# Order of the split products inside a tile of expert weights: high parts of both row halves first, then the low parts

## Chip, cores and metric

The kernel runs on one core of a Trainium2 chip. The metric is the device time of one execution in microseconds (us), given as the median of several runs. The core's engines are TensorE (PE, matrix products; PEld are its weight loads), VectorE (DVE), ScalarE (ACT), GpSimd (POOL) and SyncE (SP, which here issues DMAs).

## What is computed

The reference is one transformer block: modulation, a token mixer (neighbourhood attention beside a recurrent branch), a normalisation, and a mixture of experts with expert choice routing. The change touches the experts alone. Cut to them:

```python
N_EXPERTS = 16; CAPACITY_FACTOR = 2; D_EXPERT = 2816   # T = 1024 tokens, d = 1024
def expert_choice_ffn(u, w_router, w1, w3, w2):
    cap = CAPACITY_FACTOR * T // N_EXPERTS                # 128 tokens per expert
    aff = jax.nn.softmax(u @ w_router, axis=-1)
    gate, idx = lax.top_k(jnp.swapaxes(aff, 1, 2), cap)
    xs = jax.vmap(lambda ub, ib: ub[ib])(u, idx)
    hdn = silu(einsum('becd,edf->becf', xs, w1)) * einsum('becd,edf->becf', xs, w3)
    ye = einsum('becf,efd->becd', hdn, w2) * gate[..., None]
    return scatter_add(ye, idx)
```

Each of the 16 experts has 128 tokens, two up projections of 1024 x 2816 and one down projection of 2816 x 1024, all in float32.

## The kernel before

**Tiling.** The expert stage is the function `moe`. The 2816 hidden columns of an expert are cut into three chunks `FC` of 1024, 1024 and 768 columns. A step is one chunk of one matrix: (e, ci, 1) for `w1`, (e, ci, 3) for `w3`, (e, ci, 2) for `w2`. The down step of a chunk stands one chunk late, after the two up steps of the next. A step is cut into units, each of two blocks of 128 rows of the weight ("row halves", k = 2q and 2q+1): four units for an up step, four (or three, for 768) for a down step. That makes 35 units per expert and 560 in all. An up unit of the last chunk is 768 columns wide, the others are 1024 wide.

**From memory to the products.** `load(u)` (L878) issues the DMA of unit u into one of 13 `raw` buffers on SP's queue. `split(u)` writes the weights as a sum of two tiles: ScalarE casts the high part `hi` (L884), and VectorE subtracts it from `raw` to get the low part `lo` (L885). `hi` and `lo` each come from a ring of three buffers (`HLB=3`), and a buffer is free again when its last reader is done. The activations are split in the same way, into `xh` and `xl` for the up steps and `dh` and `dl` for the down steps. A product is then three matmuls: high by high, high activation by low weight, and low activation by high weight. The weight tile is the moving operand, the activation block of 128 x 128 is the stationary one, and a row of 1024 columns makes two matmuls of 512 (for 768, one of 512 and one of 256). So a unit is twelve matmuls: L986 for the up steps, into the accumulators `ph`, and L1001 for the down steps, into `ye`.

**Around the products.** After the last unit of a `w1` step ScalarE takes SiLU of `ph` into `hd` (L989), after `w3` VectorE multiplies `hd` (L991). TensorE transposes `hd` (L1023), ScalarE and VectorE split it into `dh` (L1024) and `dl` (L1025). At the end of an expert VectorE scales `ye` into `yo` (L1006), and GpSimd adds it into `acc` in memory (L1008). During an expert the next one is prepared: one-hot rows `oh` (L826), token numbers `idx` (L832), a gather, transposes (L850) and the split of the activations (L853 to L857). Near the end of the last expert `final(t)` (L947 to L971) normalises and stores the output rows on ScalarE, VectorE and GpSimd.

**What sets the order.** The program is written unit by unit: splits two units ahead (`LA`), loads twelve ahead (`LD`), then the unit's matmuls. A planner in the compiler places the instructions of each engine by the program's order and its own estimate of when inputs and buffers are ready. Each engine then runs its list in that fixed order.

Of the kernel before, what the change touches and what calls it, by code (L numbers as in the profile page):

```python
# [98 lines left out]
def ln_stats(nc, pool, t, mh_t, eps=LN_EPS, at=None):  # L99

    st=pool.tile([128,2,6],F32,name="bst",bufs=3) if at is None else at[:,:12].rearrange("p (s c) -> p s c",s=2)
    for s in range(2): nc.vector.bn_stats(st[:,s,:], t[:,s*512:(s+1)*512])
    mv=pool.tile([128,4],F32,name="bmv",bufs=3) if at is None else at[:,12:16]
    nc.vector.bn_aggr(mv[:,0:2], st)
    nc.vector.tensor_scalar_add(mv[:,2:3], mv[:,1:2], eps)
    nc.gpsimd.tensor_tensor(mv[:,3:4], mv[:,2:3], mh_t, op=ALU.pow)
    return mv[:,0:1], mv[:,3:4]
# [628 lines left out]
def moe(ctx, tc, K, get_t1, mc, i, G, out):  # L736
    nc=tc.nc
# [28 lines left out]
    with ExitStack() as c1:  # L766
# [6 lines left out]
        for t in range(NT):  # L773
            r=slice(t*128,(t+1)*128)
            x=get_t1(t,p)
# [16 lines left out]
            st=nc.sync.dma_start(table[r,:D],x)  # L792
# [28 lines left out]
    NC_=len(FC)  # L821

    def prep(e):
        oh=ep.tile([128,NT,128],BF16,name="oh",bufs=1)
        for t in range(NT):
            oi=nc.vector.tensor_scalar(oh[:,t,:],iota,slotT[:,t,e:e+1],None,op0=ALU.is_equal)  # L826
            if e in (1,2): behind(P[0]["xi"],oi)
        pi=ps_t.tile([128,4,128],F32,name="pt")
        for t in range(NT):
            for j in range(2): nc.tensor.matmul(pi[:,0,:1],oh[:,t,:],tok[:,t,j:j+1],start=(t+j==0),stop=(t+j==NT))  # L830
        idx=ep.tile([128,1],I32,name="idx",bufs=3)
        ic=nc.vector.tensor_copy(idx,pi[:,0,:1])  # L832
        g=ep.tile([128,D+NE],F32,name="gath",bufs=1)
        gi=nc.gpsimd.indirect_dma_start(out=g,out_offset=None,in_=table[:,:],  # L834
            in_offset=bass.IndirectOffsetOnAxis(ap=idx[:,:1],axis=0))
        return dict(gi=gi,ic=ic,idx=idx,g=g,e=e)
# [32 lines left out]
    def load(u,after=None):  # L869
        z,q=U[u]; e,ci,m=steps[z]; f0,fw=FC[ci]  # L870
        if m==2: ap,w=w2[e,f0+q*256:f0+q*256+256,:],D
        else: ap,w=(w1 if m==1 else w3)[e,q*256:q*256+256,f0:f0+fw],fw
        j=len(RN)%(RAW0+RAWB+RAW2); RN.append(0)
        z=G["raw0"] if j<RAW0 and u<len(U)-FS+LD else raw if j<RAW0+RAWB else raw2
        if len(RN)==1: r=G["r0"]
        else:
            r=z.tile([128,2048],F32,name="raw")
            di=(nc.gpsimd if after else nc.sync).dma_start(r[:,:2*w].rearrange("p (n w) -> p n w",n=2),ap.rearrange("(k p) f -> p k f",p=128))  # L878
            if after: behind(after,di)
        SP[u]=(r,w)  # L880
    def split(u):
        r,w=SP[u]
        hi,lo=[hl.tile([128,2048],F32R,name=n) for n in ("hi","lo")]
        nc.scalar.copy(hi[:,:2*w],r[:,:2*w])  # L884
        li=nc.vector.tensor_sub(lo[:,:2*w],r[:,:2*w],hi[:,:2*w].bitcast(F32))  # L885
        if u<12: behind(P[0]["ic"],li)
        SP[u]=[(hi[:,k*w:(k+1)*w],lo[:,k*w:(k+1)*w]) for k in range(2)]
    with tc.tile_pool(name="m2",bufs=2,side="right") as p:
# [34 lines left out]
        w=lambda n: p.tile([128,2,128],F32,name=n,bufs=1)  # L923
# [22 lines left out]
    def scale_shift(x,nm,rs,op):  # L946
        nc.vector.scalar_tensor_tensor(x,x,nm,g2row,op0=op,op1=ALU.mult)  # L947
        nc.vector.scalar_tensor_tensor(x,x,rs,b2row,op0=ALU.mult,op1=ALU.add)
# [25 lines left out]
    for u,(s,q) in enumerate(U):  # L974
        e,ci,m=steps[s]; last=q==nu(ci,m)-1
        for n in range(SN,min(u+LA+1,len(U))): split(n); SN=n+1
        if u+LD<len(U): load(u+LD)
        d=P[e]; w=SP.pop(u); f0,fw=FC[ci]; nf=fw//128
        if m!=2:
            if q==0: PH[m]=[ps_h.tile([128,512],F32,name=f"ph{m}{j}") for j,_ in halves(fw)]  # L980
            xh,xl=d["xh"],d["xl"]
            for k in (2*q,2*q+1):
                wh,wl=w[k%2]
                for x,y,a,b in ((xh,wh,True,False),(xh,wl,False,False),(xl,wh,False,True)):
                    for j,c in halves(fw):
                        nc.tensor.matmul(PH[m][j][:,:c.stop-c.start],x[:,k,:],y[:,c],start=(k==0 and a),stop=(k==7 and b))  # L986
            if last and m==1:
                hd=ep.tile([128,1024],F32,name="hd",bufs=1)
                for j,c in halves(fw): nc.scalar.activation(hd[:,c],PH[1][j][:,:c.stop-c.start],AF.Silu)  # L989
            elif last:  # L990
                for j,c in halves(fw): nc.vector.tensor_mul(hd[:,c],hd[:,c],PH[3][j][:,:c.stop-c.start])  # L991
                HD[e,ci]=hd
        else:
            if ci==0 and q==0: YE[e]=[ps_y.tile([128,512],F32,name=f"ye{j}") for j in range(2)]
            ye=YE[e]; dh,dl=DH[e,ci]
            for k in (2*q,2*q+1):
                st=(ci==0 and k==0); sp=(ci==NC_-1 and k==nf-1)
                wh,wl=w[k%2]
                for l,rr,a,b in ((dh,wh,True,False),(dh,wl,False,False),(dl,wh,False,True)):
                    for j in range(2):  # L1000
                        nc.tensor.matmul(ye[j],l[:,k,:],rr[:,j*512:(j+1)*512],start=st and a,stop=sp and b)  # L1001
            if ci==NC_-1 and last:
                yo=ep.tile([128,D],F32,name="yo",bufs=1)
                for j in range(2):
                    c=slice(j*512,(j+1)*512)
                    nc.vector.scalar_tensor_tensor(yo[:,c],ye[j],d["gate"],gt2row[:,c],op0=ALU.mult,op1=ALU.mult)  # L1006
                if e<NE-1:
                    nc.gpsimd.indirect_dma_start(out=acc[:,:],out_offset=bass.IndirectOffsetOnAxis(ap=d["idx"][:,:1],axis=0),  # L1008
                        in_=yo,in_offset=None,compute_op=ALU.add)
                else:  # L1010
                    nc.vector.tensor_add(yo,yo,ag);
                    nm,rs=ln_stats(nc,None,yo,mh,at=Q[:,0,:16])
                    scale_shift(yo,nm,rs,ALU.subtract)

        nxt=steps[s+1] if s+1<len(steps) else None
        for key in list(HD) if last else ():
            if m==2 or (m==3 and (nxt is None or nxt[2]!=2)) or (nxt==(key[0],key[1],2)):
                ee,cc=key; fw2=FC[cc][1]; nf2=fw2//128
                hd=HD.pop(key)
                dh=ep.tile([128,8,128],F32R,name="dh",bufs=1); dl=ep.tile([128,8,128],F32R,name="dl",bufs=1)  # L1020
                for k0 in range(0,nf2,4):
                    n=min(4,nf2-k0); ks=slice(k0,k0+n); pt=ps_t.tile([128,4,128],F32,name="pt")
                    for k in range(n): nc.tensor.transpose(pt[:,k,:],hd[:,(k0+k)*128:(k0+k+1)*128],ident)  # L1023
                    nc.scalar.copy(dh[:,ks],pt[:,:n])  # L1024
                    nc.vector.tensor_sub(dl[:,ks],pt[:,:n],dh[:,ks].bitcast(F32))  # L1025
                DH[key]=(dh,dl)
        if last and m==1 and ci==0 and e+1<NE: P[e+1]=prep(e+1)
        if q==1 and m!=2 and ci==NC_-1 and e+1<NE: prep2(P[e+1],(m//2,))
        if u==len(U)-FS:
            ag=ep.tile([128,D+NE],F32,name="gath",bufs=1)[:,:D]  # L1030
            nc.gpsimd.indirect_dma_start(out=ag,out_offset=None,in_=acc[:,:],in_offset=bass.IndirectOffsetOnAxis(ap=P[NE-1]["idx"][:,:1],axis=0))
            gb=G["raw0"].tile([128,2048],F32,name="raw"); g2row,b2row=gb[:,:D],gb[:,D:]
            for z,n in ((g2row,2),(b2row,3)): nc.sync.dma_start(z,i["lnrows"][n:n+1,:].to_broadcast([128,D]))
        for t in range(NT):
            if u==len(U)-XE[t]: final(t)
# [4 lines left out]
def body(tc, i, out):  # L1040
    nc = tc.nc
    with ExitStack() as ctx:
        cp = ctx.enter_context(tc.tile_pool(name="c", bufs=1))
        ident = cp.tile([128, 128], F32, name="ident")
        make_identity(nc, ident)
        mh = cp.tile([128, 1], F32, name="mh")
        nc.gpsimd.memset(mh, -0.5)
        G = dict(pool=cp, ctx=ctx, ident=ident, mh=mh)
        mc = ExitStack()
        cm = mixer(ctx, tc, i, G, lambda: moe_keep(ctx, tc), mc)  # L1050
        K = G["keep"]
        get = merge_top(mc, tc, i, G, cm)
        moe(ctx, tc, K, get, mc, i, G, out)
# [17 lines left out]
```

## Time and profile before

| | us |
|---|---|
| median of 3 runs | 3240.75 (3239.29 to 3241.23) |
| the profiled execution | 3231.57 |
| its span, first to last instruction | 3229.8 |
| TensorE busy | 2986.9 (92%) |
| VectorE busy | 2359.8 (73%) |
| ScalarE busy | 1730.5 (54%) |

Busy times are sums over the span. TensorE's matmuls are pipelined and their ends are modelled, so the distance between the starts of matmuls tells more than their durations. Idle time in brackets in a timeline stands before the instruction, with what ended it. Weight loads (PEld) are listed apart from the matmuls and run beside them.

### The profile page before, as it was taken

To read this page: it belongs to the slowest core of one execution; us is meant where nothing else is said; L and a number is where in the kernel's file an instruction comes from. 1 tells how busy PE (TensorE), PEld (TensorE's weight loads), DVE (VectorE), ACT (ScalarE), POOL (GpSimd) and SP (SyncE) were. 2 spreads that over 40 slices of the span, in tenths; PEclk is the share of its full clock that TensorE was granted. 3 is DMA by queue.
4 is the path that set the end of the run, shared out by engine and by line. 5 is a ranking of instruction groups with operands and counts; after the bars stand their busy time and mean duration, and the time that the engine had idled before them with its cause. 6 is when DMAs were issued, how large, how long until landed. Compare 5 with 4: busy or idle time off the path is not lost.

```text
span 3229.8 us, 47355 instructions
## 1 busy us (share of the span) xinstructions
PE 2986.9 (92%) x17884; PEld 2367.9 (73%) x17884; DVE 2359.8 (73%) x3206; ACT 1730.5 (54%) x1996; POOL 637.6 (20%) x509
## 2 busy tenths in 40 slices
PE   7998989998879978999879999999999999999995
PEld 3777767776667764577658888888888878888884
DVE  4335545543566767757789889888888888888887
ACT  3343333433224343432357777777777777777775
POOL 2233333333231326311000000111010111010004
PEclk9999999998789999999889999999999999999998
DMA  5245444455768876544589999999999999999985
GB/s 192 86 129 135 124 113 121 127 143 132 170 171 206 187 179 207 154 160 151 182 324 383 387 372 370 357 363 375 381 362 363 357 365 376 381 362 363 363 318 227
DMA packets 537368, 825.17 MB, mean 255 GB/s; under 512 B 206318, under 2 KB 335470, under 8 KB 537012
## 3 DMA queue, kind: packets, MB, share of 16 engines
q1 hardware_dynamic: 489308, 742.36, 67.1%
q10 hardware_dynamic: 42472, 60.25, 5.8%
q0 software_dynamic: 5360, 19.54, 2.3%
q8 instruction: 141, 2.31, 0.3%
q14 instruction: 87, 0.71, 0.1%
HBM read 732.48 MB, written 89.55 MB: 255 GB/s over the span
## 4 chain that ended last, share of the span: by engine, by line
PE 42%; DVE 9%; DMA 4%; issue 4%; ACT 2%; POOL 1%; ACTq 0%; POOLq 0%; DVEq 0%; SPq 0%
PE ph L986 21%; PE ye L1001 13%; DVE lo L885 4%; PE pA L679 3%; DMA raw<-in_w_e_dram 2%; PE po L722 2%; PE pt L1023 1%; ACT hi L884 1%; DMA bt<-in_bias_dram 1%; DVE dl L1025 1%; DVE oh L826 0%; PE pl L798 0%; PE yp L583 0%; PE apt L576 0%; ACT xh L856 0%
## 5 line engine op out<-in xcount | busy, mean ns | idle before, releaser
L885 DVE TENSOR_TENSOR lo<-raw,hi 128x2048 fp32r<-128x2048 f32 (+1 forms) x560 | 1197.6, 2170 | 107.8 <-ACT hi L884 91.7
L884 ACT CAST hi<-raw 128x2048 fp32r<-128x2048 f32 (+1 forms) x560 | 1010.0, 1814 | 353.6 <-PE ph L986 191.3
L986 PE MATMUL ph<-lo,xh 128*128 128x512 f32 (+1 forms) x1536 | 456.6, 378 | 23.3 <-DVE lo L885 22.9
L986 PE MATMUL ph<-hi,xh 128*128 128x512 f32 (+1 forms) x1536 | 448.7, 374 | 3.1 <-ACT xh L856 2.0
L986 PE MATMUL ph<-hi,xl 128*128 128x512 f32 (+1 forms) x1536 | 448.3, 373 | 0.0
L986 PEld LDWEIGHTS ph<-lo,xh 128*128 128x128 f32 x1536 | 267.5, 188 | 95.3 <-DVE lo L885 48.3
L986 PEld LDWEIGHTS ph<-hi,xh 128*128 128x128 f32 x1536 | 271.5, 188 | 56.1 <-ACT xh L856 2.4
L986 PEld LDWEIGHTS ph<-hi,xl 128*128 128x128 f32 x1536 | 270.8, 188 | 52.6
L228 PE MATMUL pp<-uh,whi 128*128 128x512 f32 (+1 forms) x832 | 265.7, 392 | 5.4 <-DVE th L304 3.1
L228 PE MATMUL pp<-ul,whi 128*128 128x512 f32 (+1 forms) x832 | 266.1, 388 | 0.0
L228 PE MATMUL pp<-uh,wlo 128*128 128x512 f32 (+1 forms) x832 | 263.1, 386 | 0.0
L834 POOL DMA_INDIRECT gath<-table,idx x16 | 37.8, 2364 | 958.5 <-DVE oh L826 587.7
L1001 PE MATMUL ye<-lo,dh 128*128 128x512 f32 x704 | 222.5, 397 | 1.2 <-DVE lo L885 1.2
L1001 PE MATMUL ye<-hi,dl 128*128 128x512 f32 x704 | 218.9, 392 | 3.3 <-DVE dl L1025 3.3
L1001 PE MATMUL ye<-hi,dh 128*128 128x512 f32 x704 | 219.6, 393 | 2.4 <-ACT hi L884 1.3
L228 PEld LDWEIGHTS pp<-uh,whi 128*128 128x128 f32 x832 | 154.6, 196 | 41.7 <-issue 8.1
L228 PEld LDWEIGHTS pp<-uh,wlo 128*128 128x128 f32 x832 | 155.8, 195 | 36.9 <-issue 7.5
L228 PEld LDWEIGHTS pp<-ul,whi 128*128 128x128 f32 x832 | 155.7, 195 | 36.6 <-issue 8.5
L262 DVE TENSOR_TENSOR tmp<-AU,W 120x144 f32<-120x144 f32 (+24 forms) x248 | 92.3, 372 | 117.5 <-DMA AU<-aD 73.5
L216 POOL TENSOR_TENSOR wlo<-wraw,whi 128x512 fp32r<-128x512 f32 x86 | 113.3, 1337 | 226.8 <-ACT whi L215 186.4
L1001 PEld LDWEIGHTS ye<-hi,dl 128*128 128x128 f32 x704 | 132.8, 189 | 32.2 <-DVE dl L1025 3.8
L1001 PEld LDWEIGHTS ye<-hi,dh 128*128 128x128 f32 x704 | 131.1, 189 | 30.6 <-ACT hi L884 2.0
(331 smaller groups left out, 4484.3 us busy)
## 6 DMA issues: line engine op xcount, KB each, us to landing
raw<-in_w_e_dram SPq DMA_DIRECT2D x430, 1024.0 KB
raw<-in_w_e_dram SPq DMA_DIRECT2D x128, 768.0 KB
wraw<-in_w_in_dram SPq DMA_DIRECT2D x86, 256.0 KB
wmod<-in_w_mod_dram SPq DMA_DIRECT2D x48, 256.0 KB
BTD<-BT SPq DMA_DIRECT2D x40, 256.0 KB
cBT<-BTD SPq DMA_DIRECT2D x40, 256.0 KB
wmod<-in_w_mod_dram SPq DMA_DIRECT2D x8, 1024.0 KB
XD<-X SPq DMA_DIRECT2D x32, 256.0 KB
```

What stands on the lines that cost most here:

```text
L216: nc.gpsimd.tensor_sub(l[:,ks],r,h[:,ks].bitcast(F32))
L228: nc.tensor.matmul(p,wt[:,k,:],ut[:,k,a:a+b],start=(k==0 and first),stop=(k==7 and last))
L262: nc.vector.tensor_tensor(v,AU[d][:,:,s,ts_][:,:,None,:].to_broadcast([120,2,nj,L]), W[d][:,:,js,s:s+1].to_broadcast([120,2,nj,L]),op=ALU. ...
L679: nc.tensor.matmul(pq[q],w[:,kk,:],y[:,kk,q*512:(q+1)*512],start=(kk==0 and first),stop=(kk==3 and last))
L722: nc.tensor.matmul(pq[q],a[:,r],w[:,q*512:(q+1)*512],start=(k==0 and first),stop=(k==7 and last))
L834: gi=nc.gpsimd.indirect_dma_start(out=g,out_offset=None,in_=table[:,:], in_offset=bass.IndirectOffsetOnAxis(ap=idx[:,:1],axis=0))
L884: nc.scalar.copy(hi[:,:2*w],r[:,:2*w])
L885: li=nc.vector.tensor_sub(lo[:,:2*w],r[:,:2*w],hi[:,:2*w].bitcast(F32))
L986: nc.tensor.matmul(PH[m][j][:,:c.stop-c.start],x[:,k,:],y[:,c],start=(k==0 and a),stop=(k==7 and b))
L1001: nc.tensor.matmul(ye[j],l[:,k,:],rr[:,j*512:(j+1)*512],start=st and a,stop=sp and b)
L1023: for k in range(n): nc.tensor.transpose(pt[:,k,:],hd[:,(k0+k)*128:(k0+k+1)*128],ident)
L1025: nc.vector.tensor_sub(dl[:,ks],pt[:,:n],dh[:,ks].bitcast(F32))
```

## The change

In a unit, the loop over the two row halves and the loop over the three products change places. Before, the first half takes high by high, high by low and low by high, then the second half does. After, both halves take high by high, then both take the low part of the activation by the high part of the weight, and then both take the high part of the activation by the low part of the weight. The number of matmuls, their operands and the accumulators stay as they are.

```diff
-            for k in (2*q,2*q+1):
-                wh,wl=w[k%2]
-                for x,y,a,b in ((xh,wh,True,False),(xh,wl,False,False),(xl,wh,False,True)):
+            for x,l,a,b in ((xh,0,True,False),(xl,0,False,False),(xh,1,False,True)):
+                for k in (2*q,2*q+1):
                     for j,c in halves(fw):
-                        nc.tensor.matmul(PH[m][j][:,:c.stop-c.start],x[:,k,:],y[:,c],start=(k==0 and a),stop=(k==7 and b))
+                        nc.tensor.matmul(PH[m][j][:,:c.stop-c.start],x[:,k,:],w[k%2][l][:,c],start=(k==0 and a),stop=(k==7 and b))
...
-            for k in (2*q,2*q+1):
-                st=(ci==0 and k==0); sp=(ci==NC_-1 and k==nf-1)
-                wh,wl=w[k%2]
-                for l,rr,a,b in ((dh,wh,True,False),(dh,wl,False,False),(dl,wh,False,True)):
+            for z,l,a,b in ((dh,0,True,False),(dl,0,False,False),(dh,1,False,True)):
+                for k in (2*q,2*q+1):
+                    st=(ci==0 and k==0); sp=(ci==NC_-1 and k==nf-1)
                     for j in range(2):
-                        nc.tensor.matmul(ye[j],l[:,k,:],rr[:,j*512:(j+1)*512],start=st and a,stop=sp and b)
+                        nc.tensor.matmul(ye[j],z[:,k,:],w[k%2][l][:,j*512:(j+1)*512],start=st and a,stop=sp and b)
```

## Rows read from the trace of the kernel before

**Rows 1.** The page: busy time by engine, and TensorE's busy tenths in 40 slices.

```profile
PE 2986.9 (92%) x17884; PEld 2367.9 (73%) x17884; DVE 2359.8 (73%) x3206; ACT 1730.5 (54%) x1996; POOL 637.6 (20%) x509
...
PE   7998989998879978999879999999999999999995
```

**Rows 2.** Chain of waits, one piece per expert: start us, us, what.

```profile
1915.17 7.74 PE ye L1001 x34
2010.25 7.74 PE ye L1001 x34
...
2983.05 7.74 PE ye L1001 x34
3079.39 7.74 PE ye L1001 x34
```

**Rows 3.** Stretches of one expert: busy us (count) by engine, granted clock, DMA share, GB/s.

```profile
1915.20:2010.20 95.00, 94.78 (x467) 78.64 (x467) 86.19 (x65) 70.60 (x54) 4.23 (x3) 1.00 1.00 377
2593.90:2691.20 97.30, 95.74 (x468) 78.58 (x467) 86.59 (x65) 70.95 (x54) 8.24 (x3) 1.00 0.98 368
```

**Rows 4.** Waits, 2593.9 to 2691.2, the last row 1915.2 to 2010.2: us, times, longest.

```profile
PEld ph L986 <- DVE lo L885: 3.6, 5, 0.9
...
PE ph L986 <- DVE lo L885: 1.4, 4, 0.5
...
PEld ph L986 <- DVE lo L885: 0.3, 2, 0.2
```

**Rows 5.** Timeline of TensorE at two stalls: start us, us, line, tiles, idle before.

```profile
2636.53 0.61 PE L986 MATMUL ph<-hi,xh 128*128 128x512 f32 x2
2637.52 0.74 PE L986 MATMUL ph<-lo,xh 128*128 128x512 f32 x2 [0.37 <-DVE lo L885]
2638.10 0.63 PE L986 MATMUL ph<-hi,xl 128*128 128x512 f32 x2
...
2639.96 0.62 PE L986 MATMUL ph<-hi,xh 128*128 128x512 f32 x2
2640.92 0.72 PE L986 MATMUL ph<-lo,xh 128*128 128x512 f32 x2 [0.34 <-DVE lo L885]
```

**Rows 6.** Timeline of TensorE without a stall, and a group of weight loads.

```profile
2596.07 0.62 PE L1001 MATMUL ye<-hi,dh 128*128 128x512 f32 x2
2596.52 0.61 PE L1001 MATMUL ye<-lo,dh 128*128 128x512 f32 x2
2596.97 0.62 PE L1001 MATMUL ye<-hi,dl 128*128 128x512 f32 x2
2597.43 0.62 PE L1001 MATMUL ye<-hi,dh 128*128 128x512 f32 x2
...
L986 PEld LDWEIGHTS ph<-hi,xh 128*128 128x128 f32 x96 | 16.9, 188 | 3.3
```

**Rows 7.** One cast, one subtraction; group of casts, 2593.9 to 2691.2: busy, mean ns | idle.

```profile
2610.40 1.91 ACT L884 CAST hi<-raw 128x2048 fp32r<-128x2048 f32 x1 [1.35 <-PE ph L986]
...
2608.66 2.28 DVE L885 TENSOR_TENSOR lo<-raw,hi 128x2048 fp32r<-128x2048 f32 x1
...
L884 ACT CAST hi<-raw 128x2048 fp32r<-128x2048 f32 (+1 forms) x36 | 65.1, 1816 | 22.6 <-PE ph L986 12.2 <-PE ye L1001 10.3
```

**Rows 8.** Timeline of TensorE at a stall in the chunk of 768 columns.

```profile
2682.16 0.50 PE L986 MATMUL ph<-hi,xh 128*128 128x512 f32 x2
2683.21 0.62 PE L986 MATMUL ph<-lo,xh 128*128 128x512 f32 x2 [0.54 <-DVE lo L885]
```

**Rows 9.** A stretch of 2 us, as rows 3, and SP's queue, 2593.9 to 2691.2.

```profile
2490.00:2492.00 2.00, 2.00 (x14) 1.74 (x13) 2.00 (x2) 1.29 (x2) 0.00 (x0) 1.00 1.03 422
...
SPq L878 <- DVE lo L885: 77.6, 33, 4.4
```

**Rows 10.** Waits of TensorE, 3079.4 to 3180, and one row of its timeline.

```profile
PE ph L986 <- DVE lo L885: 5.8, 6, 1.5
...
3199.11 1.22 PE L1001 MATMUL ye<-hi,dl 128*128 128x512 f32 x2 [3.33 <-DVE dl L1025]
```

## Prediction

> **What bounds the kernel now.** I read the page first. TensorE is busy for 92% of the span, VectorE for 73%, and the slices show where TensorE is full: from slice 22 to slice 39, the expert stage, TensorE stands at 9 in every slice [rows 1]. The change touches only this stage, so I left the first half aside. Next I took the chain of work that ended last. It shows the same piece, 34 down products (L1001), once per expert; from 2010.25 to 2983.05 us that is ten periods in 972.8 us, 97.28 us each, while the one before them, 1915.17 to 2010.25, took 95.08 [rows 2]. Both do the same work, so 2.2 us per expert is waiting. The table of stretches agrees: in the short period TensorE is busy 94.78 of 95.00 us, in the long ones 95.7 of 97.30, at a granted clock of 1.00, that is at the 2.4 GHz level [rows 3].
>
> Then the waits say what TensorE waits for. In one long period the weight loads of L986 wait five times, 3.6 us in all, for VectorE's `lo` (L885), and the matmuls 1.4 us; no wait of TensorE for `hi` stands among them. In the short period it is 0.3 us for L986 [rows 4]. ScalarE, in turn, stands idle 22.6 us before its casts, 12.2 and 10.3 of it until TensorE is done: it waits for a slot of the ring of three, not for weights. So the order of the stage is: TensorE frees a `hi` slot, ScalarE casts (1.91 us), VectorE subtracts (2.28 us) [rows 7], and TensorE needs `lo` two matmuls into the unit. TensorE is the bound, and the late feeder behind it is VectorE.
>
> **What a stall costs.** The timeline of TensorE shows matmuls in pairs. Undisturbed pairs start 0.455 us apart, 0.2275 us per matmul of 512 columns [rows 6]. Where `lo` is late, the pair on `hi` at 2636.53 is followed by the first pair on `lo` only at 2637.52, 0.99 us later, and the next pair comes 0.58 us after that: 0.535 + 0.125 us lost. The next unit loses 0.505 the same way (2639.96, 2640.92) and again some 0.11 after it [rows 5]. In the third chunk of an expert a pair is 512 + 256 columns and starts 0.35 us apart; there the stall from 2682.16 to 2683.21 loses 0.70, and some 0.11 after it [rows 8]. These are three of the five stalls of this expert; the other two repeat the pattern at 2610.99 and 2614.18 and lose 0.46 and 0.41. The five sum to 2.95 us, so a period without them would be 97.28 - 2.95 = 94.3 us. The short period of 95.08 still has some waits for `lo`, so 94.3 beside it is plausible.
>
> **The change part by part.** Nothing is added or removed: each unit has the same twelve matmuls, each with its own weight load, on the same two halves of PSUM. No DMA and no instruction of another engine is issued elsewhere in the code. Three moments move.
>
> (1) The first use of `lo` goes from the third matmul of a unit to the ninth. That is 6 x 0.2275 = 1.365 us of cover in a unit of 1024 columns, and three pairs, 3 x 0.35 = 1.05 us, in one of 768. The steady stalls are smaller, even when two units in a row are added up because VectorE carries its lateness over: 0.535 + 0.125 + 0.505 + 0.11 = 1.27 us against 1.365; 0.87 for the other couple; 0.81 against 1.05. So each of the five should go, if VectorE does its work in the same order.
>
> (2) The last use of `hi` goes from the twelfth matmul to the eighth, so its slot comes free 4 x 0.2275 = 0.91 us sooner (0.70 in a narrow unit). ScalarE waits for just that slot [rows 7], so cast, subtraction and the release of the raw buffer may all come up to 0.91 us sooner. I count nothing for it by itself; it is the reserve for the tight couple in (1).
>
> (3) The last use of `lo` goes from the tenth matmul to the twelfth, 0.455 us later. VectorE writes this slot only after ScalarE's cast, which starts at the eighth matmul at the earliest and takes 1.91 us [rows 7], while the slot is free 0.91 us after the eighth. This costs nothing, between zero and zero, as long as the cast takes over 0.91 us.
>
> The low parts of the activations, `xl` and `dl`, are needed at the fifth matmul before and after, so they don't move. What is late next: VectorE works 86.6 us per expert, 92% of 94.3, and ScalarE 71.0 [rows 3]. Neither becomes the bound, but VectorE has 0.4 us to spare per unit, so a burst of other VectorE work must be carried by the cover. Memory: at 368 GB/s over 97.3 us an expert moves 35.8 MB; 94.3 us wants 380 GB/s. The trace has 377 over a whole period without a TensorE wait, and 422 in a stretch of 2 us, and SP stands waiting for VectorE to free raw buffers 77.6 us of 97.3 [rows 3, 9]. So it keeps up.
>
> The sum: ten steady periods at 2.95 give 29.5 us. I take 28, since the planner places the instructions anew and some stall may survive; its ends are 0 and 29.5. The expert from 2983.05 to 3079.39 took 96.34 [rows 2], 2.0 above 94.3; I take 2. The three before 2010 are 0.7 above it each, 2.1 in all; I take 1. Behind 3079 the waits of TensorE are larger, 5.8 us for `lo` [rows 10], because ScalarE and VectorE also do the final normalisation there; `hi` is late there too, which isn't helped, and a wait of 3.3 us for `dl` stays [rows 10]; I take 3, ends 0 and 8. The sum is 28 + 2 + 1 + 3 = 34 us (ends 0 and 42). The profiled execution took 3231.57 us, with a span of 3229.8; the median of the runs is 3240.75, 9.2 above it. The stage is the same in both, so I take 34 off either: 3197.6 profiled, and a median of 3240.75 - 34 = 3206.8.
>
> **The rivals.** (a) VectorE takes the place of the stall: with TensorE faster, the bursts of one-hot, `dl`, `xl` and output work come closer together, or the planner puts VectorE's instructions in another order, and half of the stalls survive or return elsewhere. For it: VectorE at 89% and the couple that leaves 0.1 us. Against it: (2), and VectorE's idle time, 97.3 - 86.6 = 10.7 us per expert [rows 3], in which it catches up. Price: about half of the sum, 17 us, 3224.
>
> (b) Memory becomes the bound at what the first experts show: 377 GB/s gives 35.8 / 0.377 = 95.0 us per expert, ten times 2.3 saved and 4 at the end, 3214. Against it: the 422 GB/s stretch and SP's waits.
>
> (c) Slower: the change of stationary operand. Before, a unit changes it four times (four matmuls on `xh`, two on `xl`, twice); after, six times. If loading a repeated operand were cheap and a changed one had to be paid, two more changes x 560 units x 0.188 us, the time of a load, would be 211 us more, 3452 less the stalls, 3418. It decides from 34 / 1120 = 30 ns per change. Against it: pairs start 0.45 to 0.46 us apart whether the operand stays (`hi,dh` to `lo,dh`) or changes (`lo,dh` to `hi,dl`, `hi,dl` to `hi,dh`) [rows 6]; the difference is below 10 ns, and a load stands before each matmul in any case.
> The Trainium skill has a rule on this side, in "TensorE: Matmul & The Clock Gate", the section on packing small matmuls: a weight load overlaps running matmuls only when the row group differs, which no full-array load here does. By it each changed load would be exposed, and the time would be that of (c). The trace disagrees: loads of 188 ns each [rows 6] stand beside matmuls that start every 227 ns.
>
> (d) No effect: the planner moves matmuls of other units in between, so `lo` is met as early as before, or the waits sit on something that comes with `lo`. 3240.75.
>
> **How the numbers follow.** Forecast 0.63 (3199 to 3213); (a) 0.16; (b) 0.06; (d) 0.07; (c) or another slowdown by the new order 0.05; more than 42 us saved 0.03. The predicted time is 3207. The range goes from 3198, nearly the whole sum of ends, to 3225, which takes in (a) and (b). Differences within 0.2%, 6.5 us, are about what a measurement of this kernel can't tell from no change. Faster: 0.63 + 0.16 + 0.06 + 0.03 = 0.88; the same 0.07; slower 0.05.
>
> **What would show it.** In the profile after: the period of an expert at 94.3 to 94.6 us in the chain; the waits of TensorE for `lo` of L885 gone from the steady experts; TensorE busy over 99% of them; VectorE near 92%, DMA at 378 to 380 GB/s. A pair still 0.455 us apart refutes (c); waits of TensorE for `lo` that remain, with VectorE at 93% or above, would show (a); waits of ScalarE for raw weights would show (b). Periods of 97.3 would make the prediction wrong.

## The result, and the profile after

The changed kernel is slower: 3268.55 us (median of 5 runs, 3266.49 to 3272.22), beside 3240.75 us before. The ratio is 1.0097, its 95% interval 1.0083 to 1.0112. The forecast was 3207, with a range up to 3225, so it had the wrong sign. The profiled execution after took 3266.49 us with a span of 3264.7. Against the profiled span of before that is 34.9 us; against the medians it is 27.8, because the profile of before is a run 9.2 us below its median and that of after one 2.1 below.

The page looks much like [rows 1]. TensorE has a little more busy time, in the same number of instructions, and stands at 9 in all slices of the expert stage:

```profile
PE 3008.2 (92%) x17884; PEld 2367.6 (73%) x17884; DVE 2352.8 (72%) x3206; ACT 1713.3 (52%) x1996; POOL 606.0 (19%) x509
...
PE   7998989997878978999789999999999999999995
```

So the page doesn't show where the time went. The period of an expert does. I take it as the distance between the first scaling of `ye` into `yo` (L1004 in the changed kernel, L1006 before) of one expert and that of the next:

| us | start of the first | periods | last start to the end of the span |
|---|---|---|---|
| before | 1764.70 | 95.06, 95.08, 95.31, nine of 97.22 to 97.31, 96.32, 95.80, 90.73 | 21.2 |
| after | 1767.58 | 94.26, 94.49, 97.02, nine of 99.84 to 99.92, 99.64, 99.55, 98.03 | 15.2 |

The fifteen periods add 38.0 us: the first two save 1.4, the third adds 1.7, the nine steady ones add 23.4, and the last three 14.4. The start adds 2.9 and the end saves 6.0; the sum is the 34.9 us of the spans. The first two experts run at just the 94.3 us that the prediction gave for all of them. From the fourth to the twelfth an expert takes 99.9.

Three stretches of the changed kernel, in the columns of [rows 3]: the first expert, the second, and a steady one:

```profile
1767.60:1861.85 94.25, 94.25 (x468) 78.86 (x467) 86.23 (x65) 71.26 (x53) 4.51 (x2) 1.00 1.00 378
1861.85:1956.35 94.50, 94.50 (x469) 79.07 (x468) 86.25 (x65) 71.17 (x53) 6.44 (x3) 1.00 1.01 379
2452.80:2552.70 99.90, 97.18 (x468) 78.48 (x467) 85.90 (x65) 69.45 (x53) 4.79 (x3) 1.00 0.98 355
```

VectorE (86 us) and ScalarE (69 to 71 us) have the same work in all three, TensorE has the same number of matmuls to within two, the granted clock is 1.00, and memory moves less in the slow stretch, not more. So it is no new work, no clock and no lack of bandwidth. The waits of the steady stretch (us, times, longest), beside those of [rows 4]:

```profile
ACT dh L1022 <- PE ye L999: 13.6, 3, 5.3
DVE lo L885 <- ACT hi L884: 7.6, 7, 2.8
ACT hd L988 <- PE ph L985: 6.8, 2, 3.4
ACT hi L884 <- PE ye L999: 5.7, 5, 2.1
PEld ph L985 <- DVE lo L885: 4.5, 7, 1.2
...
ACT hi L884 <- PE ph L985: 2.0, 3, 0.8
...
PEld ph L985 <- ACT hi L884: 1.1, 2, 0.7
```

Before, ScalarE's waits in an expert were at its casts: 22.6 us, for a slot [rows 7]. They are now mostly at `dh` and `hd`, 20.4 us, and only 7.7 at the casts. VectorE then waits for the casts, and TensorE for VectorE, and now for `hi` too, which it never did in the long period of before. ScalarE's timeline shows why. Of the changed kernel, first the second expert, then a steady one (in brackets the idle time before the instruction):

```profile
1859.75 1.92 ACT L884 CAST hi<-raw 128x2048 fp32r<-128x2048 f32 x1 [0.81 <-PE ye L999]
1862.01 1.07 ACT L1022 CAST dh<-pt 128x512 fp32r<-128x512 f32 x2 [0.34 <-PE ye L999]
1863.37 1.91 ACT L884 CAST hi<-raw 128x2048 fp32r<-128x2048 f32 x1 [0.29 <-PE ph L985]
...
2445.73 1.91 ACT L884 CAST hi<-raw 128x2048 fp32r<-128x2048 f32 x1 [0.81 <-PE ye L999]
2452.97 1.07 ACT L1022 CAST dh<-pt 128x512 fp32r<-128x512 f32 x2 [5.33 <-PE ye L999]
2453.93 7.33 ACT L884 CAST hi<-raw 128x2048 fp32r<-128x2048 f32 x4
2464.68 1.09 ACT L988 ACTIVATE hd<-ph 128x512 f32<-128x512 f32 x2 [3.42 <-PE ph L985]
```

And the same place in a steady expert of the kernel before:

```profile
2242.21 1.92 ACT L884 CAST hi<-raw 128x2048 fp32r<-128x2048 f32 x1 [1.70 <-PE ye L1001]
2244.48 1.08 ACT L1024 CAST dh<-pt 128x512 fp32r<-128x512 f32 x2 [0.35 <-PE ye L1001]
```

Before, `dh` comes to the head of ScalarE's list when TensorE is nearly there, and costs 0.35 us. After, it stands there 5.33 us before it can start. It does not wait for its input, as TensorE's timeline shows:

```profile
2448.26 1.03 PE L1021 MATMUL pt<-ident,hd 128*128 128x128 f32 x8
...
2451.86 1.07 PE L999 MATMUL ye<-lo,dh 128*128 128x512 f32 x4
```

The transposes of `hd` are over more than 3 us before `dh` starts. But the program gives `dh` one buffer (`bufs=1`), and the down products of the chunk before read it until the second row. Wherever `dh` waits for TensorE in these kernels, it starts 0.43 us after the start of the last matmul that reads the old `dh`. The casts behind it could have gone: four of them follow in one piece without a gap, so at least the first had a slot and weights waiting. ScalarE works its list in order, so the casts wait behind `dh`.

How far the casts are ahead can be counted: at the start of each `dh` and `hd`, the casts already done less the units that TensorE has begun (a unit partly done counts by its matmuls). I call this the lead. Before, it is 1.9 to 2.1 at every first `dh` and `hd` of a steady expert. After, it is 2.6 to 2.9 in the first two experts, where nothing stalls, and 0.9 to 1.4 in the steady ones. Same program text, another place in the list: this is the planner's order, not the chip's. Counted in ScalarE's list itself, all six stand one to three casts earlier than in the first two experts. Beside the kernel before, three of the six stand one cast earlier; at the other three the place is the same, and TensorE is 0.6 to 0.8 of a unit further on when they start. With a lead of 1, ScalarE then has to make up for several casts at once, and TensorE feels it:

```profile
2526.11 1.07 PE L985 MATMUL ph<-hi,xh 128*128 128x512 f32 x4
2527.02 1.07 PE L985 MATMUL ph<-hi,xl 128*128 128x512 f32 x4
2528.91 1.21 PE L985 MATMUL ph<-lo,xh 128*128 128x512 f32 x4 [0.82 <-DVE lo L885]
```

The first two rows are eight matmuls, 0.91 us for four. The low part, now needed only at the ninth, still comes about 1 us late (1.89 us from 2527.02 to 2528.91, in place of 0.91), 8.9 us after a `dh` that started at 2520.03 with 4.68 us of idle time before it. Summed from the distances of the starts, TensorE loses about 6.0 us in this expert: 3.68 in eight stalls for `lo`, 0.59 in two for `hi`, the rest in small gaps, many of 0.11 us right behind a stall. Before it lost about 3.4, 2.36 of it in five stalls. The difference is the 2.6 us by which the period grew.

The loads were not late: SP's queue stood waiting for VectorE to free raw buffers for most of the stretch, as in [rows 9].

```profile
SPq L878 <- DVE lo L885: 66.4, 31, 5.9
```

### The profile page after: what moved, and what is told of

The parts are those of the page before. It is cut to its first block, busy times and chain, and to the rows that moved or that the text cites. A ratio compares the mean times of both kernels' runs of the same rounds, so it can differ in the third digit from the quotient of the medians.

```text
span 3264.7 us, 47321 instructions
## 1 busy us (share of the span) xinstructions
PE 3008.2 (92%) x17884; PEld 2367.6 (73%) x17884; DVE 2352.8 (72%) x3206; ACT 1713.3 (52%) x1996; POOL 606.0 (19%) x509
## 5 line engine op out<-in xcount | busy, mean ns | idle before, releaser
L884 ACT CAST hi<-raw 128x2048 fp32r<-128x2048 f32 (+1 forms) x560 | 993.5, 1814 | 205.3 <-PE ye L999 86.0
L985 PE MATMUL ph<-lo,xh 128*128 128x512 f32 (+1 forms) x1536 | 394.5, 379 | 22.6 <-DVE lo L885 19.2
L985 PE MATMUL ph<-hi,xh 128*128 128x512 f32 (+1 forms) x1536 | 397.2, 379 | 9.1 <-ACT hi L884 6.7
L985 PE MATMUL ph<-hi,xl 128*128 128x512 f32 (+1 forms) x1536 | 389.4, 374 | 0.0
L834 POOL DMA_INDIRECT gath<-table,idx x16 | 19.8, 1237 | 994.2 <-DVE idx L832 846.1
L999 PE MATMUL ye<-lo,dh 128*128 128x512 f32 x704 | 195.2, 399 | 7.5 <-DVE lo L885 7.5
L999 PE MATMUL ye<-hi,dl 128*128 128x512 f32 x704 | 191.0, 393 | 6.8 <-DVE dl L1023 6.8
L999 PE MATMUL ye<-hi,dh 128*128 128x512 f32 x704 | 190.7, 393 | 1.9 <-ACT dh L1022 1.9
```

Of the source, the lines that this page charges most:

```text
L985: nc.tensor.matmul(PH[m][j][:,:c.stop-c.start],x[:,k,:],w[k%2][l][:,c],start=(k==0 and a),stop=(k==7 and b))
L999: nc.tensor.matmul(ye[j],z[:,k,:],w[k%2][l][:,j*512:(j+1)*512],start=st and a,stop=sp and b)
```

## Experiments

The theory: the product order itself gains what was forecast, but the planner moved ScalarE's `hd` and `dh` (and VectorE's work that follows) to a lead of one cast, and this costs more. The rivals: the new order as such loses on the chip (memory, VectorE, stationary operands), or the early release of `hi` does. In the diffs `behind(a,b)` is an ordering rule of the program: it has the planner place `b` after `a` in the list of their engine. `HI[u]` and `LO[u]` are the cast and the subtraction of unit u.

**Only ScalarE's places, new products.** The SiLU and `dh` are put behind the cast two units on.

```diff
-nc.scalar.activation(hd[:,c],...)
+behind(HI[min(u+2,len(U)-1)],nc.scalar.activation(hd[:,c],...))
-nc.scalar.copy(dh[:,ks],pt[:,:n])
+behind(HI[min(u+2,len(U)-1)],nc.scalar.copy(dh[:,ks],pt[:,:n]))
```

> The changed kernel, with one more rule for the planner: the SiLU into hd (L989) and the casts into dh stand on ScalarE behind the cast of hi two units on, as they stand in the kernel before. Theory A (the slowdown is ScalarE's fixed order: from the fourth expert on hd and dh stand one cast too early and hold up casts whose slot is free, ScalarE idles 3.4 to 5.3 us at them): the later periods fall from 99.9 us to 95 to 97, the median from 3268 to 3205 to 3235. Theory B (the new product order itself loses once the first loads are used up, through the ring or through memory at 357 GB/s): no effect, 3262 to 3274.

Measured 3235.36 us (10 runs), ratio 0.9987 to before (0.9977 to 0.9998): about the time of before, and 33 us below the changed kernel. ScalarE's `hd` and `dh` now have, place by place, the list of the kernel before, while the transposes on TensorE stay where the changed kernel has them. Two lines that touch no product take the whole loss away, but don't bring the gain. Periods settle at 97.5, so time and period lie just above what was expected. `dh` and `hd` now have a lead of 1.9 to 2.0, but for one `hd` and one `dh` at 1.2, and still wait, as these waits of one expert (2351.5 to 2449.1) show:

```profile
ACT dh L1023 <- PE ye L1000: 7.9, 3, 3.6
...
ACT hd L989 <- PE ph L986: 4.0, 2, 2.5
...
PEld ph L986 <- DVE lo L885: 2.7, 5, 0.8
```

The places that were right before are too early now: `dh` waits 7.9 us in an expert, beside 1.9 before. An estimate for the `dh` of the last chunk: a `hi` slot comes free 0.91 us sooner, which brings ScalarE to `dh` sooner, and the last product that reads the old `dh` is the twelfth matmul of its unit in place of the tenth, 0.455 us later. That is 1.37 us, and this wait grew from 0.35 to 1.72. The other two grew by 2.2 and 2.4; what the rest of that is was not followed up.

**Three casts ahead, and VectorE's places too.** The split is written three units ahead, `hd` and `dh` go behind the cast three units on, and on VectorE the `hd` product, `dl` and `yo` behind the subtraction two units on.

```diff
-RAWB,RAW2,HLB,L0,L1,LD,LA=9,3,3,8,10,12,2
+RAWB,RAW2,HLB,L0,L1,LD,LA=9,3,3,8,10,12,3
...
+behind(HI[min(u+3,len(U)-1)],nc.scalar.copy(dh[:,ks],pt[:,:n]))
+behind(LO[min(u+2,len(U)-1)],nc.vector.tensor_sub(dl[:,ks],pt[:,:n],dh[:,ks].bitcast(F32)))
```

> The changed kernel, with splits written three units ahead, hd and dh behind the cast three units on, and on VectorE hd, dl and yo behind the subtraction two units on: the order that the planner itself chose for the first three experts of the changed kernel, where a period takes 94.3 us. Theory A: 94.3 to 95 us per expert throughout, median 3198 to 3215, below the kernel before. Theory B: 3262 to 3274.

Measured 3219.41 (4 runs), ratio 0.9939 (0.9921 to 0.9956): faster than before, 4 us above the expected range. (Only the first two experts of the changed kernel took 94.3 us, not three; the third took 97.02.) Periods settle at 96.1. What is left stands in the waits of one expert (2344.99 to 2441.11):

```profile
DVE idx L832 <- PE pt L830: 3.5, 1, 3.5
ACT yo L854 <- PE pt L850: 2.9, 1, 2.9
...
PEld ph L986 <- DVE lo L885: 2.2, 5, 0.6
...
ACT dh L1023 <- PE ye L1000: 0.9, 1, 0.9
```

`dh` hardly waits any more. Two other instructions now stand at the head of a list too early, both of the next expert's preparation. This run moves ScalarE's places and VectorE's together, so it doesn't tell what each is worth.

**The preparation placed as well.** The one before, with the one-hot rows, `xf`, `xh` and `xl` under the same rules, and `idx` written three units later.

```diff
+    def oA(x):
+        if ORD[0] is not None: behind(HI[min(ORD[0]+3,len(U)-1)],x)
+    def oD(x):
+        if ORD[0] is not None: behind(LO[min(ORD[0]+2,len(U)-1)],x)
...
-            nc.scalar.copy(xh[:,c],xf[:,c])
+            oA(nc.scalar.copy(xh[:,c],xf[:,c]))
...
+        if m==3 and q==2 and ci==0 and e+1<NE: P[e+1]=prepb(e+1,PB)
```

> As e2, and the preparation of the next expert is placed too: its one-hot rows, xf, xh and xl stand behind the cast three units on or the subtraction two units on, and idx is written three units later, so that VectorE does not wait for it. Theory A (what is left of the loss in e2, 96.1 us per expert against 94.3, is again order: VectorE waits 3.4 us for idx and ScalarE 2.9 us for a transpose at the head of their lists): 94.3 to 94.8 us per expert, median 3196 to 3212. Rival (VectorE or memory is the bound at 96.1): 3215 to 3222.

Measured 3198.97 (3192.38 to 3202.2, 4 runs), ratio 0.9877 (0.9848 to 0.9906), as expected. A steady expert:

```profile
2429.84:2524.10 94.26, 94.26 (x468) 78.81 (x467) 86.28 (x65) 70.48 (x54) 8.33 (x3) 1.00 1.00 378
```

All steady periods are 94.26, TensorE loses about 0.5 us in one, and no wait of TensorE for `lo` is left in it. All weights are loaded here, so neither memory (378 GB/s) nor VectorE (86.28 of 94.26) holds the new order back.

**The same rules with the old products.** The kernel before, with rules of the same kind for the same instructions, two units on for ScalarE and VectorE alike.

```diff
-nc.scalar.copy(dh[:,ks],pt[:,:n])
+behind(HI[min(u+2,len(U)-1)],nc.scalar.copy(dh[:,ks],pt[:,:n]))
...
```

> The kernel before, old order of products, with rules of the same kind as e5, two units on instead of three since its hi buffers come free later. If the order of ScalarE and VectorE is all that matters and the order of the products nothing: as e5. If the products' new order gives cover of its own (lo needed six matmuls later): stalls for lo stay, 95.5 to 97.5 us per expert, 3215 to 3242.

Measured 3199.58 (3196.51 to 3206.84, 4 runs), ratio 0.9888 (0.9859 to 0.9917). The expectation of 3215 to 3242 was wrong: it took the stalls of [rows 5] for something that the old product order must have. It need not have them. A steady expert:

```profile
2428.33:2522.93 94.60, 94.59 (x468) 78.83 (x467) 86.29 (x65) 70.89 (x55) 4.15 (x3) 1.00 1.00 379
```

One stall of 0.17 us for `lo` is left, and the periods are 94.5 to 94.8. So with the lists in order, the change of products is worth about 0.3 us per expert, and in the total nothing that these runs can tell (3198.97 and 3199.58); the two also differ by one unit in how far ahead the splits are written. This version and the one above are the fastest of all; either beats both kernels.

**A short lead in the kernel before.** Old products, the split written one unit ahead instead of two, `hd` and `dh` in front of the cast two units on.

```diff
-RAWB,RAW2,HLB,L0,L1,LD,LA=9,3,3,8,10,12,2
+RAWB,RAW2,HLB,L0,L1,LD,LA=9,3,3,8,10,12,1
...
+        for b in LATE.pop(u-2,()): behind(b,hi_)
...
+LATE.setdefault(u,[]).append(nc.scalar.copy(dh[:,ks],pt[:,:n]))
```

> The kernel before, old order of products, with hd and dh put one cast earlier on ScalarE (splits written one unit ahead, and the cast of two units on stands behind hd and dh). Theory A: the order alone makes it slower; the subtraction two units on ends some 5.5 us after the unit and is needed 3.2 us after it, so each of the six places per expert costs about 2 us, 10 to 13 us per expert, 3380 to 3440. Theory B: the order of these few instructions does not matter, 3235 to 3250.

Measured 3430.0 (2 runs), ratio 1.059 (1.0565 to 1.0616); periods of 109.2, 12.0 us more per expert. The lead is 0.8 to 1.0. The waits of one expert (2552.06 to 2661.33) have much the same top rows as the changed kernel; the first row here is the stretch itself, as in [rows 3]:

```profile
2552.06:2661.33 109.27, 99.32 (x468) 79.41 (x467) 86.16 (x65) 70.09 (x54) 3.83 (x3) 0.98 0.91 326
...
ACT dh L1025 <- PE ye L1002: 17.9, 4, 4.8
...
PEld ph L987 <- DVE lo L886: 11.9, 7, 2.0
DVE lo L886 <- ACT hi L884: 11.0, 9, 4.1
ACT hd L990 <- PE ph L987: 10.0, 3, 4.9
```

A short lead alone, without the change, makes the same picture. It stands 14.6 us above the 94.6 that the old products take under placed lists; the changed kernel, at about the same lead, stands 5.6 above its 94.26. So the later use of `lo` seems to soften the fault. The comparison is rough, since here all splits are written a unit later, and since the granted clock is 0.98 here: in every steady expert it falls to 0.50 once, for about 3.4 us, and the longer distances of the matmuls in that time make up about 1.6 of the 12.0 us.

**Half of the loads.** The changed kernel, but only every other unit's weights are loaded, and the second unit of a pair splits the buffer of the first. So half of the weights are left out of the result.

```diff
     def load(u,after=None):
         z,q=U[u]; e,ci,m=steps[z]; f0,fw=FC[ci]
+        if q%2: SP[u]=SP[u-1]; return
```

> The changed kernel with only every other unit of weights loaded; the second unit of a pair splits the buffer of the first, so half of the weights are left out and the output is another. All casts, subtractions and products stay. The planner then keeps hd and dh three casts behind for all sixteen experts. If the planner's order is what loses time, and it changes when the planner believes itself short of loads: 94.3 us per expert throughout, 3190 to 3212. If the loss comes from the product order itself and not from loads: 99.9 us per expert, 3260 or so.

Measured 3205.07 (2 runs), ratio 0.9896 (0.9873 to 0.9919). Periods are 94.26 from the first expert to the twelfth, and the lead at `dh` and `hd` is 2.6 to 2.9 in a steady expert, as in the first two of the changed kernel. A steady expert:

```profile
2427.49:2521.74 94.25, 94.25 (x468) 78.85 (x467) 86.23 (x64) 71.26 (x53) 5.33 (x3) 1.00 0.63 201
```

Two readings are possible: the loads were late on the chip, or only in the planner's estimate. The run above with all weights at 94.26 us, and SP's waits for buffers in the changed kernel, speak against the first. So the planner's order depends on the loads, and it changes once the stock of loaded buffers is, by its estimate, used up. That last half is inferred from the orders; its estimate itself is not in a trace.

**One half of the change at a time.** First only the up steps in the new order, then only the down steps, with no rule added.

```diff
             for x,l,a,b in ((xh,0,True,False),(xl,0,False,False),(xh,1,False,True)):
                 for k in (2*q,2*q+1):
...
-            for z,l,a,b in ((dh,0,True,False),(dl,0,False,False),(dh,1,False,True)):
-                for k in (2*q,2*q+1):
+            for k in (2*q,2*q+1):
+                for l,rr,a,b in ((dh,wh,True,False),(dh,wl,False,False),(dl,wh,False,True)):
```

> The change in the up steps (L986) alone; no rules for the planner. Its order puts one hd of three one cast early, and dh stays two casts behind. Theory A: one early place instead of five or six, with the cover of the up units kept: 95.5 to 98 us per expert, 3215 to 3245. If the loss came from the new product order itself in the up steps: 3255 to 3270.

Measured 3213.92 (4 runs), ratio 0.9928 (0.9901 to 0.9954), a little better than expected; periods of 95.0 to 95.1. The lead is 1.4 to 2.1 everywhere but at one `hd` per expert, where it is 1.0, and ScalarE's timeline shows that place:

```profile
2510.66 0.60 ACT L988 ACTIVATE hd<-ph 128x512 f32<-128x512 f32 x1 [4.74 <-PE ph L985]
```

The 4.74 us at that `hd` cost TensorE only 0.32 us behind it (a stall of 0.21 and the gap after it): an up unit whose `lo` is needed at the ninth matmul carries most of it.

> The change in the down steps (L1001) alone; no rules for the planner. Its order puts one dh of three one cast early, hd stays. The stalls before stand in the up units, which keep the old order, and the early dh adds one stall of some 2 us per expert: 97.5 to 100 us per expert, 3240 to 3275. If the early place costs nothing: 3238 to 3242.

Measured 3256.32 (5 runs), ratio 1.0058 (1.0034 to 1.0081), as expected slower; periods of 98.2 and 99.6, in no fixed turn. Here it is a `dh` that comes early, with a lead of 0.9 and an idle time of 5.12 us (at 2514.18), and the up units behind it have the old order, without cover. TensorE there:

```profile
2516.70 0.45 PE L830 MATMUL pt<-tok,oh 128*128 128x1 bf16 x12
2517.02 0.71 PE L986 MATMUL ph<-hi,xh 128*128 128x512 f32 x2
2517.57 0.25 PE L830 MATMUL pt<-tok,oh 128*128 128x1 bf16 x4
2519.22 0.73 PE L986 MATMUL ph<-lo,xh 128*128 128x512 f32 x2 [1.40 <-DVE lo L885]
...
2520.41 1.05 PE L986 MATMUL ph<-hi,xh 128*128 128x512 f32 x2
2521.27 1.05 PE L986 MATMUL ph<-lo,xh 128*128 128x512 f32 x2
```

So the up half gains 26 us and the down half loses 16, while both together lose 28: the halves don't add, because the planner makes another order for each. Why the down half alone makes it put a `dh` early, no run here tells.

## Why the prediction was wrong

**The floor was right.** 94.3 us for an expert without stalls is what the first two experts after took (94.26 and 94.49), and all steady ones where the lists are in order. Where the lead was kept, the new products left no stall for `lo`, as (1) said; but with the lists in order the old products left only one of 0.17 us, so the cover was not what had been missing.

**The step that failed is the condition in (1)**, "if VectorE does its work in the same order". It was written down and then priced as if it held. It did not: the engines' lists are made anew for the changed program, and from the third expert on ScalarE's `hd` and `dh` stand at a lead of about 1 in place of 2. In the sum, the term of 28 us had ends of 0 and 29.5, "some stall may survive"; the lower end supposed that a new order can at worst give nothing. Measured, the third to the twelfth period lost 25.1 us (1.7 and nine times 2.6). A new order has no bound at zero, as the run at a short lead shows: 12 us per expert.

**(2) was counted at nothing, and is where the order turns.** The earlier release of `hi` is a gain for the chip only if ScalarE has a cast to do at that moment. With a lead of 2 it stands at `dh` instead (7.9 us in the first experiment), with 3 it doesn't (0.9 in the second). Step (2) looked at slots and not at what else is in ScalarE's list. The prediction saw ScalarE idle 22.6 us before its casts and asked only which slot it waits for. Such idle time is to spare only while nothing else at the head of the list keeps the casts back.

**A fourth moment moves.** The prediction counted three. The last product that reads `dh` goes from the tenth matmul of a unit to the twelfth, so the one buffer of `dh` comes free 0.455 us later. It is a small part of the 5.33 us, but it lengthens just the wait at which ScalarE is held. No run gave `dh` a second buffer, so whether that would do instead of the ordering rules is open.

**(3) was right in its price, not in its reason.** With all lists placed, VectorE does wait for TensorE to free a `lo` slot, 4.0 us in an expert:

```profile
DVE lo L895 <- PE ye L1010: 2.4, 1, 2.4
...
DVE lo L895 <- PE ph L996: 1.6, 2, 1.3
```

It costs nothing because VectorE is then ahead; TensorE waits for no `lo` in that expert. I had said that the slot is always free in time.

**The remaining terms.** I took 1 us for the three experts before 2010; the first two saved 1.4, the third lost 1.7. I took 2 for the one from 2983 and 3 for the last part behind 3079. The part from the last `yo` to the end did get shorter, by 6.0, but the last three periods grew by 3.3, 3.8 and 7.3. Why the last three grew by more than the steady ones was not followed up. The start of the stage came 2.9 us later; the prediction had no term for that. The 0.4 us that VectorE was said to have to spare per unit leaves out all of its work but the subtraction; with the 86.6 us of an expert it is (94.3 - 86.6) / 35 = 0.22.

**The rivals.** (a) named the planner, "puts VectorE's instructions in another order", but capped its price at half of the gain. The engine was ScalarE, with VectorE behind it, and VectorE was not busier (85.9 us). (b) fell: 378 GB/s carries 94.26 us. (c) fell: four matmuls take 0.91 us, two pairs of 0.455, with six changes of the stationary operand in a unit. The rule of the Trainium skill that the prediction quotes, from "TensorE: Matmul & The Clock Gate", the section on packing small matmuls, would by itself expose each of those loads; the same section also has loads into a background weight buffer run ahead of running matmuls. The unchanged distance speaks against the first here and does not contradict the second. What was given to "another slowdown by the new order" had a chance of at most 0.05, shared with (c), and no mechanism and no price. It is the case that came.

**The sign that was there.** The periods of before, 95.06, 95.08 and 95.31 and then 97.3, already showed one program text running at two speeds with a break after the third expert. I read the 2.2 us as a lack of cover in the unit. VectorE's timeline of before has the break in plain sight, at its product of `hd` in the first chunk of an expert, just before the end of the second and of the third period:

```profile
1946.68 1.28 DVE L991 TENSOR_TENSOR hd<-hd,ph 128x512 f32<-128x512 f32 x2
...
2041.04 1.28 DVE L991 TENSOR_TENSOR hd<-hd,ph 128x512 f32<-128x512 f32 x2 [0.97 <-PE ph L986]
```

At 2041.04 this product stands at the head of VectorE's list 0.97 us too early, with three subtractions behind it that then follow without a gap, and from there on the experts take 97.3 us. In one of these (2593.9 to 2691.2) VectorE waits for TensorE before three kinds of instructions other than the subtractions:

```profile
DVE hd L991 <- PE ph L986: 2.2, 3, 1.0
...
DVE idx L832 <- PE pt L830: 1.6, 1, 1.6
...
DVE yo L1006 <- PE ye L1001: 1.2, 1, 1.2
```

In the short period of 1915.2 to 2010.2, and in the old products under placed lists, VectorE waits for nothing but ScalarE's casts (8.8 and 8.3 us). ScalarE's `hd` and `dh` have the same places in its list in all three; the transposes on TensorE differ by up to a unit. So with the old products it was VectorE's list that the rules put right, and the 94.6 us show that most of the 2.2 us was order.

## What to carry to other kernels

Where a planner writes the engines' lists, a change of the order on one engine can change the order on all of them, and its price has no lower end at zero; before counting a gain, ask which instructions on the feeding engines wait for the changed one, for their input or for their buffer, and how many of the next feeds stand ahead of them. In the profile, look at what the feeder waits for by instruction: idle time before its own feeds was slack here, idle time before something else with feeds queued behind it was the loss. If a steady loop shows two periods, compare the lists of the fast and the slow one first; fixing the places with a few ordering rules gave 41 us here, with either order of the products.

## What the runs showed of the hardware

After a stall TensorE can pay twice. In the experts read here each of its stalls for `lo` or `hi` is followed by a gap of about 0.11 us behind the first matmul, beside the wait itself. And in the run with only the down steps changed, the granted clock fell behind the 1.40 us of waiting above: the matmuls from 2520.4 on start 0.43 us apart, in place of 0.2275, and a stretch of 1 us shows the level (columns as in [rows 3]):

```profile
2521.00:2522.00 1.00, 1.00 (x4) 0.81 (x3) 1.00 (x3) 0.00 (x0) 1.00 (x1) 0.50 0.90 319
```

0.50 is the level of 1.2 GHz. It lasted about 3.4 us, and the longer distances cost another 1.6 us, as much as the stall itself (1.54). But the fall does not come with every such stall. The expert before this one has the same stall, and the clock stays at 1.00 behind it:

```profile
2421.05 0.73 PE L986 MATMUL ph<-lo,xh 128*128 128x512 f32 x2 [1.40 <-DVE lo L885]
...
2422.00:2423.00 1.00, 1.00 (x7) 0.80 (x5) 1.00 (x1) 0.27 (x1) 1.00 (x1) 1.00 0.75 143
```

From the fourth period to the fourteenth, the six of about 99.6 us all have the fall, and the five of 98.0 to 98.2 have none, and it makes up their difference. In the run at a short lead a steady expert has three stalls with 1.59 us of waiting, and one fall, behind the first of them. In the steady experts of the changed kernel, with stalls of up to 0.99 us, the granted clock stayed at 1.00. What decides whether it falls, these runs don't tell. So a stall of TensorE should not be priced at its own length alone.
